# The first quad gathered in one run, score products over 128 rows, no scaling on GpSimd, and another branch at the end, in a two-layer hybrid network on one core

## The chip, the cores and the metric

The kernel runs on one core of a Trainium2 chip. Five engines work side by side: TensorE (PE) multiplies matrices, VectorE (DVE) and ScalarE (ACT) work element by element, GpSimd (POOL) too, and SyncE (SP) issues most of the transfers. The profile calls the queue of an engine PEq, DVEq, ACTq, POOLq and SPq, and the loading of weights into TensorE PEld. The metric is the device time of one execution in microseconds (us), a median over runs.

## The reference

One sequence of 256 tokens, 1024 wide, goes through two layers. Layer 0 mixes with stick-breaking attention and a state-space part, layer 1 with a sparse attention of three branches (compressed blocks, selected blocks, window) and 16 heads; each mixer is followed by a mixture of 16 experts, two of which serve a token, and a layer norm stands behind each step. Cut to what matters here:

```
for layer in range(2):
    m = even_mixer(h, ...) if layer == 0 else nsa_mixer(h, ...)
    h = layer_norm(ALPHA * h + m, ...)
    h = layer_norm(ALPHA * h + moe_ffn(h, ...), ...)

# nsa_mixer, of a head: two of its three branches
p = softmax(mask(q @ ks.T * scale)); o_s = p @ vs
p = softmax(mask(q @ kw.T * scale)); o_w = p @ vw
o = g0 * o_c + g1 * o_s + g2 * o_w

# moe_ffn
for e in range(16):
    y += gates[:, e:e+1] * ((silu(x @ w1[e]) * (x @ w3[e])) @ w2[e])
```

With 256 tokens the selected blocks and the window both cover every earlier token, so the two branches have the same form and differ in their keys and values.

## The kernel before, in words

The kernel runs layer 0's mixer, its experts, layer 1's mixer and its experts, in full precision. Weights come in units of 1 MB (`u` tiles, 128 x 2048), in the order in which they are used; SP issues each as soon as a buffer is free (`issue`, L144). Where a product needs more precision than one pass gives, an operand is split into a rounded part and a remainder (`split`, L192 and L195; `q_turn`, L1396 and L1397; `k_turn`, L1360 and L1362).

**Experts** (`moe`). Each expert has 64 slots. `one_hot` makes a matrix that picks the tokens of four experts (a quad), and `gather` (L469) multiplies the tokens with it, one chunk of 128 features after another: two products of 128x256 to a chunk, and a scaling into `xe` by ScalarE (L354) or VectorE (L356) in turn. `up` (L493) multiplies a quad's slots with the weights of two experts: four products of 128x512 to a chunk and matrix pair, two chunks to a unit. For the first quad the kernel before gathers two chunks, multiplies these, gathers the next two, and so on. Later quads are gathered between other work. `down` (L523) is the second expert product.

**Second attention** (`mixer1`, `head`). For each of 16 heads and each half t of the tokens, three products are added up in PSUM: queries with keys (L1504, 128 rows: 64 features and, under them, the remainders of the same 64 of `qq`), queries with the remainders of the keys (L1505, only the 64 rows of this head's side, `q[s]` and `kl[j][s]`), and the causal mask (L1506). VectorE takes the maximum (L1507), ScalarE the exponential with its sum (L1510), VectorE inverts the sum and multiplies it with the gates (L1513, L1515). Then the probabilities are scaled: for t=0 by VectorE in two pieces of 128x128 (L1522), for t=1 by GpSimd in one piece of 128x512 (L1519; the table `PSC` says which). Two heads later they are transposed (L1529, L1535), copied (L1530, L1536) and multiplied with the values (L1550).

**The end.** The output leaves by four transfers (L348). Then each engine loads a count (L1726) and branches (L1728): if an expert has more tokens than slots, the whole network runs again in a form that copes with any count. This second program stands in the instruction stream between the branch and the common end (L1741), and is not run here. SP's part of it has all the transfers of the second program.

Instructions stand in the order of the program on each engine, except that a scheduler orders VectorE, ScalarE and GpSimd around them by dependences; the stretch after the first quad holds PE to program order.

Of the kernel before, what the change touches and what calls it, by code (L numbers as in the profile page):

```python
# [38 lines left out]
WARM0 = 5  # L39
WARM2 = 2  # L40
LAG = 2
PSC = (lambda h: False, lambda h: True)
OV = 3
LATE = (8, 10)
LATE_S = 11
FIRST = 2
IN_S = 20
CT = (3, 10)
CAP = (5, 9, 19, 20, 10, 14, 12, 10)
# [2 lines left out]
class K:  # L52
# [17 lines left out]
    def restart(self, full):  # L70

        self.full = full
        self.plan, self.tiles, self.late, self.late_s, self.in_s, self.last = [], [], [], [], [], []
        self.left = []
        self.issued = self.used = 0
        self.cap = 0
        self.rest = self.n0 = None
        self.mark = None
        self.loads = None
        self.behind = self.cut = self.tail = None  # L80
        self.staged, self.to_split, self.ahead = [], 0, 2
# [49 lines left out]
    def issue(self, cap=None):  # L131

        self.cap = self.cap if cap is None else cap
        while self.issued < len(self.plan):
            if self.issued - self.used - sum(self.used <= i < self.issued for i in self.left) >= self.cap:
                break
            if self.issued in self.left:
                self.tiles.append(None)
                self.issued += 1
                continue  # L140
            t = (self.s if self.issued in self.in_s else self.u)()
            n = 1024 if self.issued in self.last else 2048
            for c in range(0, 2048, n):
                d = self.loads = self.nc.sync.dma_start(t[:, c:c + n], self.plan[self.issued][:, c:c + n])  # L144
                if self.mark is not None:
                    self.follow(d, self.mark)
            self.tiles.append(t)
            self.issued += 1

    def issue_late(self):  # L150

        i = self.late.pop(0)
        self.tiles[i] = [self.b2() for _ in range(4)]
        for j, t in enumerate(self.tiles[i]):
            self.nc.sync.dma_start(t, self.plan[i][:, j * 512:j * 512 + 512])

    def issue_s(self):

        i = self.late_s.pop(0)
        self.tiles[i] = t = self.s()  # L160
        self.nc.sync.dma_start(t, self.plan[i])

    def unit(self):
        t = self.tiles[self.used]
# [60 lines left out]
    def pack(self, name, dt, parts, t=None):  # L225

        if t is None:
            t = self.const.tile([P, sum(math.prod(sh) for sh in parts)], dt, name="c_" + name)
            setattr(self, name, t)
        d = self.nc.sync.dma_start(t, self.a[name])  # L230
# [107 lines left out]
    def ln_transpose(self, li, n, store=None):  # L338

        nc = self.nc  # L340
        hT = self.u([P, KC, T])
        for k in range(KC):
            pt = self.acc() if k in (4, 5) else self.mm()
            for t in range(2):
                nc.tensor.transpose(pt[:, t * P:(t + 1) * P], n[:, t, k * P:(k + 1) * P], self.ident)
            self.scaled(hT[:, k], pt[:, 0:T], li, k, k % 2)
            if store is not None and k % 2:
                nc.sync.dma_start(store[:, k - 1:k + 1], hT[:, k - 1:k + 1])  # L348
        return hT

    def scaled(self, o, x, li, k, on_act):
# [121 lines left out]
    def moe(self, li, layer, n, hT):  # L473
# [71 lines left out]
                nc.gpsimd.tensor_tensor(nl[:, t], n[:, t], nh[:, t].bitcast(F32), ALU.subtract)  # L545
            return nh, nl

        self.gather(li, G, ns, xe, range(FIRST))
        h1 = self.mm()
        for k in range(0, KC, 2):  # L550
            h1 = up(h1, 0, range(k, k + 2))
            if FIRST + k < KC:
                self.gather(li, G, ns, xe, range(FIRST + k, min(FIRST + k + 2, KC)))
        self.gates(layer)
        rest = []
        with self.tc.manual_schedule(engines=ORD):
# [100 lines left out]
    def s5_tables(self, load_x, room):  # L657
# [7 lines left out]
        nc.sync.dma_start(us[:, 1344:1424], self.a["s5_par"])  # L665
        load_x()
        bc = ua[:, 0:1024].rearrange("p (x a r h) -> p x a r h", x=2, a=NP, r=2)
        nc.sync.dma_start(bc, self.a["s5_bc"])
# [188 lines left out]
    def s5_kernel(self, ca, bd):  # L857

        nc, s5 = self.nc, self.s5
        nc.gpsimd.memset(bd, 0.0)  # L860
        for g in range(2):
            s = slice(g * 64, g * 64 + 64)
            nc.scalar.activation(bd[s, :, :, g * 16:g * 16 + 16], s5["bb"][s], AF.Copy)
        pk = self.mm()
        for k4 in range(4):
            for ri in range(2):
                for q in range(4):
                    pr = k4 * 4 + q
                    nc.tensor.matmul(pk[q * 32:q * 32 + 32, k4 * P:k4 * P + P], bd[:, pr, ri],
                                     ca[ri][:, pr].rearrange("p d h -> p (d h)"), start=(ri == 0), stop=(ri == 1),  # L870
                                     skip_group_check=True, tile_position=(0, q * 32))
        ks = self.b2([P, 4, P])
        nc.scalar.activation(ks.rearrange("p k n -> p (k n)"), pk, AF.Copy)
        nc.gpsimd.tensor_tensor(ks[:, :, 0:16], ks[:, :, 0:16], self.s5dd, ALU.add)
        kds = []
        for kh in range(2):
            kd = self.drp.tile([16, 16, P], F32, name=f"kd{kh}")
            nc.sync.dma_start(kd.rearrange("h (g k) n -> g h (k n)", g=8),
                                ks[:, kh * 2:kh * 2 + 2].rearrange("p k n -> p (k n)"))
            kds.append(kd)  # L880
        return kds

    def s5_toeplitz(self, kds, kts):

        for kt, kd in zip(kts, kds):
            for j in range(8):
                n = 16 * (8 - j)
                self.nc.sync.dma_start(kt[j * 16:j * 16 + 16, :, P - n:P], kd[:, :, 0:n])

    def s5_transpose(self, x, o):  # L890

# [176 lines left out]
    def mixer0(self):  # L1068
# [5 lines left out]

        def load_x():
            t = self.u()
            half = lambda c: nc.sync.dma_start(t[:, c * 1024:c * 1024 + 1024], self.plan[0][:, c * 1024:c * 1024 + 1024])
            for k in range(0, KC, 2):
                nc.sync.dma_start(xT[:, k:k + 2], self.a["xT"][:, k:k + 2])
                if k == 0:  # L1080
                    half(0)
            half(1)
# [18 lines left out]
        def u_out(j):  # L1101
            def f(ps):
                nc.scalar.activation(uS[:, :, j], ps[:, 0:T].rearrange("p (c i) -> p i c", i=8), AF.Copy)
                if j == 3:
                    ud = self.drp.tile([8, P, P], F32, name="ud")
                    nc.sync.dma_start(ud.rearrange("j a n -> a j n"), uS.rearrange("p j k c -> p j (k c)"))
                    nc.sync.dma_start(U.rearrange("p g k c -> p (g k c)"), ud.rearrange("j (h g) n -> (j h) (g n)", h=16))
            return f

        bbp = [self.u([P, 16, 8, 16]) for _ in range(2)]  # L1110
# [190 lines left out]
    def mixer1(self, hT):  # L1301
# [43 lines left out]
        kk = self.u([P, 2, 2, 2, T], F32R)  # L1345
        vh = self.u([P, 2, 1024])
        V = vh[:, 0].rearrange("p (t n) -> p t n", t=2)
        kl = [self.b2((P, 2, T), F32R) for _ in range(2)]
        rows = (slice(0, 64), slice(64, P))

        turned = {}
# [4 lines left out]
        def k_turn(t):  # L1356
            pt = self.turn(turned["k", t]).rearrange("p (b j) n -> p j b n", b=2)
            n = slice(t * P, t * P + P)
            for c, s in enumerate(rows):
                nc.scalar.activation(kk[s, c, :, :, n], pt[s], AF.Copy)  # L1360
                for j in range(2):
                    v.tensor_tensor(kl[j][s, :, n], pt[s, j], kk[s, c, j, :, n].bitcast(F32), ALU.subtract)  # L1362
                nc.scalar.activation(kk[rows[1 - c], c, :, :, n], pt[s], AF.Copy)

        js = [self.job_T(xs, window(i)) for i in (1, 2, 3)] + self.jobs_tok(xs, k_out, self.acc)
# [121 lines left out]
        hd = {}  # L1487

        def head(i, c):
            j, s = i // 4, slice(c * 64, c * 64 + 64)  # L1490
            h = i * 2 + c
# [7 lines left out]
            for t in range(2):  # L1499
# [2 lines left out]
                z3 = z[:, 0:2 * n].rearrange("p (b n) -> p b n", b=2)  # L1502
                q = qq[j][:, c, i % 4, t * P:t * P + P]
                nc.tensor.matmul(z3, q, kk[:, c, j, :, 0:n], start=True, stop=False, skip_group_check=True)  # L1504
                nc.tensor.matmul(z3, q[s], kl[j][s, :, 0:n], start=False, stop=False, skip_group_check=True)  # L1505
                nc.tensor.matmul(z3[:, :, t * P:t * P + P], self.identb, self.caus, start=False, stop=True, skip_group_check=True)  # L1506
                v.tensor_reduce(mx[:, 2 * t:2 * t + 2], z3, AX.X, ALU.max, negate=True)  # L1507
                p_ = self.b2((P, 2, T)) if t else p0
# [5 lines left out]
            s2 = sm.rearrange("p (t b) -> p t b", t=2)  # L1514
            v.tensor_tensor(s2, s2, gt[:, :, h, 1:3], ALU.mult)  # L1515
            for t in range(2):
                x, n, pool = pr[t], P * (t + 1), PSC[t](h)
                if pool:
                    nc.gpsimd.tensor_tensor(x, x, sm[:, 2 * t:2 * t + 2, None].broadcast_to([P, 2, n]), ALU.mult)  # L1519
                    continue  # L1520
                for b in range(2):
                    v.tensor_scalar(x[:, b], x[:, b], sm[:, 2 * t + b:2 * t + b + 1], None, ALU.mult)  # L1522
            hd[h] = (pr, PT)

        def turn_p(h):
# [196 lines left out]
def body(ctx, tc, a, out):  # L1722
# [2 lines left out]
    network(k, a, out)  # L1725
    v = nc.values_load(k.mxi[0:1, 0:1], min_val=0, max_val=T,  # L1726
                       skip_runtime_bounds_check_because="a count of tokens, only compared")
    with tc.If(v > LIMIT):  # L1728

        k.restart(True)  # L1730
        network(k, a, out)
# [20 lines left out]
```

## Time and profile before

| | us |
|---|---|
| median of 3 runs | 756.65 (756.63 to 759.73) |
| profiled execution | 759.68 |
| its span | 757.8 |
| PE busy | 733.8 (97%) |
| DVE busy | 333.1 (44%) |
| ACT busy | 207.5 (27%) |
| POOL busy | 46.8 (6%) |

The span runs from the first to the last instruction of one profiled execution; the time of that execution contains it. The page gives busy time by engine, the span in 40 slices and the costliest groups of instructions with the idle time ahead of them. Here the chain of work that ended last is of no use: it consists of ScalarE's queue alone. More is to be had from the timeline of a stretch, which has the start of each instruction or run of like instructions, and from busy time by stretch.

### The profile page before, as it was taken

How to read it: one execution, taken by the hardware profiler on the slowest of the kernel's cores; microseconds unless marked ns; L12 is line 12 of the kernel's file. 1: busy time of each engine (PE TensorE's matmuls, PEld its weight loads, DVE VectorE, ACT ScalarE, POOL GpSimd, SP SyncE). 2: the span in 40 equal slices, each digit the busy share in tenths (PEclk: the TensorE clock that was granted, in tenths of full speed). 3: DMA queues.
4: the chain of work that ended last, by engine and by line, in shares of the span. 5: the costliest groups of instructions: out<-in, count | busy, mean ns of one | idle time of the engine just before them, and what ended most of it. 6: DMA issues, size and time to landing. Idle time of an engine off the chain costs nothing. (4 is left out here: it accounts for less than half of the span.)

```text
span 757.8 us, 10531 instructions
## 1 busy us (share of the span) xinstructions
PE 733.8 (97%) x4115; PEld 413.9 (55%) x4115; DVE 333.1 (44%) x849; ACT 207.5 (27%) x422; POOL 46.8 (6%) x45
## 2 busy tenths in 40 slices
PE   7999999999999999999999999999999999999993
PEld 6588777634334335334878665687535335343332
DVE  9995667512112112115855897835212112221123
ACT  1345443212101001003534675732211001011002
POOL 2010000002000000000020241300002000000000
PEclk9999999999999999999999998999999999999998
DMA  8838999799999999999982100398799999999941
GB/s 321 299 119 147 398 372 402 256 347 387 381 425 421 421 422 421 420 416 422 420 338 106 57 1 1 135 387 308 233 376 395 393 421 421 422 420 421 421 185 60
DMA packets 42539, 241.00 MB, mean 318 GB/s; under 512 B 8144, under 2 KB 9680, under 8 KB 15568
## 3 DMA queue, kind: packets, MB, share of 16 engines
q1 hardware_dynamic: 42480, 240.23, 80.7%
q8 instruction: 34, 0.56, 0.3%
q14 instruction: 25, 0.20, 0.1%
HBM read 238.38 MB, written 1.84 MB: 317 GB/s over the span
## 5 line engine op out<-in xcount | busy, mean ns | idle before, releaser
L493 PE MATMUL mm<-u,s 128*64 128x512 f32 x960 | 214.3, 595 | 0.0
L493 PEld LDWEIGHTS mm<-u,s 128*64 128x64 f32 x960 | 66.7, 137 | 129.6 <-issue 122.3
L523 PE MATMUL mm<-u,b 128*64 128x512 f32 x512 | 113.1, 593 | 0.0
L528 ACT ACTIVATE b<-mm,gslot 128x512 fp32r<-128x512 f32 x32 | 22.0, 687 | 259.0 <-PE mm L523 259.0
L529 DVE SCALAR_TENSOR_TENSOR b<-mm,gslot,b 128x512 fp32r<-128x512 f32 x32 | 24.0, 751 | 146.2 <-ACT b L528 146.2
L523 PEld LDWEIGHTS mm<-u,b 128*64 128x64 f32 x512 | 36.3, 137 | 72.0 <-issue 70.8
L195 DVE TENSOR_TENSOR s<-u,s 128x1024 fp32r<-128x1024 f32 x37 | 45.8, 1248 | 27.9 <-ACT s L192 26.3
L572 DVE TENSOR_TENSOR b<-b,mm 128x256 f32<-128x256 f32 x32 | 12.0, 417 | 92.0 <-PE mm L493 92.0
L192 ACT ACTIVATE s<-u 128x1024 fp32r<-128x1024 f32 x37 | 38.7, 1056 | 42.0 <-PE acc L205 28.9
L986 PE MATMUL mm<-u,u 128*128 128x256 f32 x208 | 46.7, 382 | 2.5 <-DMA u<-w_in 2.4
L986 PEld LDWEIGHTS mm<-u,u 128*128 128x128 f32 x208 | 38.9, 190 | 9.6 <-issue 2.4
L354 ACT ACTIVATE s<-mm,c_k_all 128x256 f32<-128x256 f32 x32 | 18.1, 564 | 81.8 <-PE mm L469 81.8
L469 PE MATMUL mm<-b,u 128*128 128x256 f32 x160 | 39.0, 325 | 0.0
L203 PE MATMUL acc<-s,u 128*128 128x512 f32 x96 | 38.0, 396 | 0.5 <-ACT u L1206 0.5
L205 PE MATMUL acc<-s,u 128*128 128x512 f32 x96 | 37.8, 394 | 0.0
L204 PE MATMUL acc<-s,u 128*128 128x512 f32 x96 | 37.5, 391 | 0.0
L534 PE MATMUL acc<-b,b 128*128 128x512 f32 x128 | 33.6, 399 | 0.1
L469 PEld LDWEIGHTS mm<-b,u 128*128 128x128 f32 x160 | 29.9, 190 | 6.4 <-issue 4.9
L592 DVE COPY b<-mm 128x512 f32<-128x512 f32 x16 | 11.1, 692 | 46.4 <-PE mm L591 46.2
L356 DVE TENSOR_SCALAR s<-mm,c_k_all 128x256 f32<-128x256 f32 x32 | 16.8, 542 | 22.9 <-PE mm L469 22.7
L534 PEld LDWEIGHTS acc<-b,b 128*128 128x128 f32 x128 | 22.5, 189 | 8.0 <-issue 3.2
L469 PE MATMUL mm<-b,s 128*128 128x256 f32 x96 | 23.5, 286 | 0.0
(312 smaller groups left out, 998.8 us busy)
## 6 DMA issues: line engine op xcount, KB each, us to landing
u<-moe SPq DMA_DIRECT2D x180, 1024.0 KB, 12.5
u<-w_in SPq DMA_DIRECT2D x26, 1024.0 KB, 16.2
u<-w_in SPq DMA_DIRECT2D x10, 512.0 KB, 6.9
s<-moe SPq DMA_DIRECT2D x4, 1024.0 KB, 5.7
b<-moe SPq DMA_DIRECT2D x16, 256.0 KB, 8.1
u<-moe SPq DMA_DIRECT2D x8, 512.0 KB, 16.9
u<-xT SPq DMA_DIRECT2D x4, 256.0 KB, 5.6
out<-u SPq DMA_DIRECT2D x4, 256.0 KB, 4.4
```

The source lines that it names most:

```text
L192: a = self.nc.scalar.activation(s[:, 0], x, AF.Copy)
L195: self.mark = self.nc.vector.tensor_tensor(s[:, 1], x, s[:, 0].bitcast(F32), ALU.subtract)
L203: mm(o, l[0], r[0], start=first, stop=False, skip_group_check=True)
L204: mm(o, l[0], r[1], start=False, stop=False, skip_group_check=True)
L205: self.tail = mm(o, l[1], r[0], start=False, stop=last, skip_group_check=True)
L469: nc.tensor.matmul(pg[:, 0:T], x[:, t, k * P:(k + 1) * P], g.bitcast(F32) if m == 1 else g, start=(i == 0), stop=(i == 2 * m - 1))
L493: self.mark = nc.tensor.matmul(h[c * 64:(c + 1) * 64], xe[:, k, e + c], w[c], start=(k == 0), stop=(k == KC - 1))
L523: self.mark = nc.tensor.matmul(y[c * 64:(c + 1) * 64], hx[:, f, c * 64:(c + 1) * 64], w[:, c * 512:c * 512 + 512], start=(f == 0), stop=(f ...
L528: nc.scalar.activation(yh, y, AF.Copy, scale=gs)
L529: nc.vector.scalar_tensor_tensor(yl, y, gs, yh.bitcast(F32), ALU.mult, ALU.subtract)
L534: self.tail = nc.tensor.matmul(out[half][t], sT[:, t * P:(t + 1) * P], yy, start=False, stop=(p == 7 and j == 1), skip_group_check=True)
L986: self.mark = self.nc.tensor.matmul(ps, w[:, k * P:k * P + P], xT[:, k], start=(k == 0), stop=(k == KC - 1))
```

## The change

Four edits, in the words of the diff. In the expert stage the first quad's eight chunks are gathered in one run, and the eight `up` steps follow. In `mixer1` the remainders of the keys, `kl`, lie in one tile of 128 rows with zeros in the other head's 64 rows (two memsets on GpSimd), so that L1505 runs over all 128 rows; `k_turn`'s subtraction takes both branches at once. `PSC` goes: the probabilities of t=1 are scaled by VectorE, in two pieces of 128x256 for each head. And the second program's transfers are issued by GpSimd's queue (`self.q`), with the branch laid out so that the path that is run here falls through.

```
-PSC = (lambda h: False, lambda h: True)
-FIRST = 2
...
     def restart(self, full):
         self.full = full
+        self.q = self.nc.gpsimd if full else self.nc.sync
...
-                d = self.loads = self.nc.sync.dma_start(t[:, c:c + n], self.plan[self.issued][:, c:c + n])
+                d = self.loads = self.q.dma_start(t[:, c:c + n], self.plan[self.issued][:, c:c + n])
...
-        self.gather(li, G, ns, xe, range(FIRST))
-        h1 = self.mm()
-        for k in range(0, KC, 2):
-            h1 = up(h1, 0, range(k, k + 2))
-            if FIRST + k < KC:
-                self.gather(li, G, ns, xe, range(FIRST + k, min(FIRST + k + 2, KC)))
+        self.gather(li, G, ns, xe, range(KC))
+        h1 = up(self.mm(), 0, range(KC))
...
-        kl = [self.b2((P, 2, T), F32R) for _ in range(2)]
+        kl = self.u([P, 2, 2, 2, T], F32R)
+        for c in range(2):
+            nc.gpsimd.memset(kl[(1 - c) * 64:(1 - c) * 64 + 64, c].bitcast(F32), 0.0)
...
-                for j in range(2):
-                    v.tensor_tensor(kl[j][s, :, n], pt[s, j], kk[s, c, j, :, n].bitcast(F32), ALU.subtract)
+                v.tensor_tensor(kl[s, c, :, :, n], pt[s], kk[s, c, :, :, n].bitcast(F32), ALU.subtract)
...
-                nc.tensor.matmul(z3, q[s], kl[j][s, :, 0:n], start=False, stop=False, skip_group_check=True)
+                nc.tensor.matmul(z3, q, kl[:, c, j, :, 0:n], start=False, stop=False, skip_group_check=True)
...
             for t in range(2):
-                x, n, pool = pr[t], P * (t + 1), PSC[t](h)
-                if pool:
-                    nc.gpsimd.tensor_tensor(x, x, sm[:, 2 * t:2 * t + 2, None].broadcast_to([P, 2, n]), ALU.mult)
-                    continue
                 for b in range(2):
-                    v.tensor_scalar(x[:, b], x[:, b], sm[:, 2 * t + b:2 * t + b + 1], None, ALU.mult)
+                    v.tensor_scalar(pr[t][:, b], pr[t][:, b], sm[:, 2 * t + b:2 * t + b + 1], None, ALU.mult)
...
-    with tc.If(v > LIMIT):
+    with tc.If(v > LIMIT, preferred_fallthrough_block=False):
```

The other `nc.sync.dma_start` of the second program's steps become `self.q.dma_start` in the same way. Line numbers after the change are one to nine lower than before: L469 becomes L468, L493 L492, L1522 L1513, L1530 L1521, L1728 L1719.

PE in the first quad of layer 1's experts before: gather products (two to a row, one chunk) and expert products (four to a row) alternate; `mm_4179` is the first pair of experts, `s_4170` the gathered tokens.

```order
L469 MATMUL mm_4171<-b_730_4167,u_3999 128x256 x2
L469 MATMUL mm_4175<-b_730_4167,u_3999 128x256 x2
L493 MATMUL mm_4179<-u_2800,s_4170 64x512 x4
L469 MATMUL mm_4186<-b_730_4167,u_3999 128x256 x2
L469 MATMUL mm_4190<-b_730_4167,u_3999 128x256 x2
L493 MATMUL mm_4179<-u_2838,s_4170 64x512 x4
L469 MATMUL mm_4200<-b_730_4167,u_3999 128x256 x2
```

The same place after:

```order
L468 MATMUL mm_4184<-b_729_4180,u_4012 128x256 x2
L468 MATMUL mm_4188<-b_729_4180,u_4012 128x256 x2
...
L468 MATMUL mm_4212<-b_729_4180,u_4012 128x256 x2
L492 MATMUL mm_4216<-u_2801,s_4183 64x512 x4
L492 MATMUL mm_4216<-u_2839,s_4183 64x512 x4
L492 MATMUL mm_4216<-u_2961,s_4183 64x512 x4
```

The eight rows of gather products now stand together, ahead of all expert products of the first pair.

DVE in the attention before, around the scalings of one head (`u_3196` its probabilities of t=0, `sm_538` its factors):

```order
L1513 RECIPROCAL sm_538_3198<-sm_538_3198 128x4
L1507 TENSOR_REDUCE mx_544_3229<-acc_3231 128x2
L1515 TENSOR_TENSOR sm_538_3198<-sm_538_3198,b_451_2581 128x4
L1507 TENSOR_REDUCE mx_544_3229<-acc_3238 128x2
L1522 TENSOR_SCALAR u_3196<-u_3196,sm_538_3198 128x128 x2
L1530 COPY u_3136<-mm_3251 128x2x128
```

And after (`b_540` is the head's probabilities of t=1):

```order
L1508 RECIPROCAL sm_537_3197<-sm_537_3197 128x4
L1502 TENSOR_REDUCE mx_543_3229<-acc_3231 128x2
L1510 TENSOR_TENSOR sm_537_3197<-sm_537_3197,b_451_2581 128x4
L1502 TENSOR_REDUCE mx_543_3229<-acc_3238 128x2
L1513 TENSOR_SCALAR u_3195<-u_3195,sm_537_3197 128x128 x2
L1513 TENSOR_SCALAR b_540_3210<-b_540_3210,sm_537_3197 128x256 x2
L1521 COPY u_3133<-mm_3252 128x2x128
```

Two scalings of 128x256 stand behind the two of 128x128; the rows around them keep their order.

SP at the end before: behind the branch stands the second program, with all its transfers.

```order
L1726 TENSOR_LOAD mxi
L1728 COMPARE_AND_BRANCH
L665 DMA u_5312<-s_par 128x80
L1079 DMA u_5306<-xT 128x512
L1077 DMA u_5316<-w_in 128x1024
```

And after:

```order
L1717 TENSOR_LOAD mxi
L1719 COMPARE_AND_BRANCH
L1719 UNCONDITIONAL_BRANCH
L614 COMPARE_AND_BRANCH
L614 UNCONDITIONAL_BRANCH x2
```

A second, unconditional branch follows the first, and what it jumps over on SP holds a loop's control and no transfer.

## Rows read from the trace of the kernel before

**Rows 1.** The page's costly groups: out<-in xcount, busy us, mean ns, idle before.

```profile
L493 PE MATMUL mm<-u,s 128*64 128x512 f32 x960 | 214.3, 595 | 0.0
...
L354 ACT ACTIVATE s<-mm,c_k_all 128x256 f32<-128x256 f32 x32 | 18.1, 564 | 81.8 <-PE mm L469 81.8
```

**Rows 2.** Busy by stretch: us, PE, PEld, DVE, ACT, POOL (instructions), clock, DMA share, GB/s.

```profile
428.00:460.00 32.00, 31.00 (x188) 19.59 (x184) 30.63 (x78) 22.30 (x80) 10.55 (x12) 0.97 0.01 5
460.00:492.00 32.00, 31.77 (x204) 20.21 (x204) 25.98 (x73) 20.59 (x81) 8.98 (x9) 0.92 0.19 73
...
458.00:465.00 7.00, 7.00 (x29) 3.76 (x30) 5.26 (x15) 2.94 (x13) 1.04 (x1) 0.51 0.00 0
```

**Rows 3.** The output's transfers (line L348): ns min/median/max, first and last start.

```profile
L348 SPq DMA_DIRECT2D out<-u x4: 343/376/396, 747.2 to 748.6; - x4
...
DMA to landing us min/median/max: 2.2/4.4/4.5
```

**Rows 4.** SP's instructions of lines L1728 and L1741, the latter by two stretches.

```profile
L1728 SPq EVENT_SEMAPHORE  x8: 17/17/17, 753.3 to 753.8; - x8
...
L1728 SPq COMPARE_BRANCH  x1: 50/50/50, 750.0 to 750.0; - x1
...
L1741 SPq EVENT_SEMAPHORE  x3: 27/28/28, 753.9 to 754.0; - x3
...
L1741 SPq EVENT_SEMAPHORE  x9: 28/28/28, 756.3 to 756.8; - x9
```

**Rows 5.** Timeline around 456 us: start, us, engine, line, in brackets idle before, releaser.

```profile
456.10 0.38 PE L1504 MATMUL acc<-u,u 128*128 128x256 f32 x1 [1.00 <-DVE u L1397]
```

**Rows 6.** Timeline of PE in the first quad of layer 1's experts.

```profile
536.27 1.99 PE L469 MATMUL mm<-b,u 128*128 128x256 f32 x8
...
543.86 1.99 PE L469 MATMUL mm<-b,u 128*128 128x256 f32 x8
```

**Rows 7.** Timeline of PE where either kind runs unbroken.

```profile
545.78 8.80 PE L493 MATMUL mm<-u,s 128*64 128x512 f32 x40
554.41 1.89 PE L493 MATMUL mm<-b,s 128*64 128x512 f32 x8
...
36.03 13.98 PE L986 MATMUL mm<-u,u 128*128 128x256 f32 x64
```

**Rows 8.** Timeline of PE at the scores of one head, t=1 and then t=0.

```profile
448.06 0.48 PE L1504 MATMUL acc<-u,u 128*128 128x512 f32 x1
448.47 0.49 PE L1505 MATMUL acc<-b,u 64*128 64x512 f32 x1
448.90 0.28 PE L1506 MATMUL acc<-c_k_bits 128*128 128x256 bf16 x1
448.93 0.36 PE L1504 MATMUL acc<-u,u 128*128 128x256 f32 x1
449.23 0.38 PE L1505 MATMUL acc<-b,u 64*128 64x256 f32 x1
449.54 0.28 PE L1506 MATMUL acc<-c_k_bits 128*128 128x256 bf16 x1
```

**Rows 9.** Timeline of PE in the output projection behind the attention.

```profile
498.33 0.40 PE L204 MATMUL acc<-s,u 128*128 128x512 f32 x1
498.57 0.39 PE L205 MATMUL acc<-s,u 128*128 128x512 f32 x1
```

**Rows 10.** Groups of DVE and POOL from 424 to 496 us, shapes kept apart.

```profile
L1522 DVE TENSOR_SCALAR u<-u,sm 128x128 f32<-128x128 f32 x32 | 17.9, 593 | 0.1
...
L1519 POOL TENSOR_TENSOR b<-b,sm 128x512 f32<-128x512 f32 x16 | 16.7, 1046 | 47.7 <-DVE sm L1515 36.5 <-ACT u L1536 5.2 <-ACT u L1510 4.1
```

**Rows 11.** Two scalings in DVE's timeline, and line L1062: ns min/median/max, shapes.

```profile
436.74 0.27 DVE L1522 TENSOR_SCALAR u<-u,sm 128x128 f32<-128x128 f32 x1
...
466.54 0.19 DVE L1522 TENSOR_SCALAR u<-u,sm 128x128 f32<-128x128 f32 x1
...
L1062 DVE TENSOR_SCALAR b<-b x3: 295/426/428, 97.2 to 396.8; 128x512 f32<-128x512 f32 x2, 128x256 f32<-128x256 f32 x1
```

More of the change, by code (lines that the diff above doesn't have):

```diff
@@ L154, in issue_late @@
         for j, t in enumerate(self.tiles[i]):
-            self.nc.sync.dma_start(t, self.plan[i][:, j * 512:j * 512 + 512])
+            self.q.dma_start(t, self.plan[i][:, j * 512:j * 512 + 512])
     def issue_s(self):
@@ L160, in issue_s @@
         self.tiles[i] = t = self.s()
-        self.nc.sync.dma_start(t, self.plan[i])
+        self.q.dma_start(t, self.plan[i])
     def unit(self):
@@ L229, in pack @@
             setattr(self, name, t)
-        d = self.nc.sync.dma_start(t, self.a[name])
+        d = self.q.dma_start(t, self.a[name])
         if self.loads is not None:
@@ L347, in ln_transpose @@
             if store is not None and k % 2:
-                nc.sync.dma_start(store[:, k - 1:k + 1], hT[:, k - 1:k + 1])
+                self.q.dma_start(store[:, k - 1:k + 1], hT[:, k - 1:k + 1])
         return hT
@@ L664, in s5_tables @@
         c8 = us[:, 1392:1424]
-        nc.sync.dma_start(us[:, 1344:1424], self.a["s5_par"])
+        self.q.dma_start(us[:, 1344:1424], self.a["s5_par"])
         load_x()
         bc = ua[:, 0:1024].rearrange("p (x a r h) -> p x a r h", x=2, a=NP, r=2)
-        nc.sync.dma_start(bc, self.a["s5_bc"])
+        self.q.dma_start(bc, self.a["s5_bc"])
         lr, li, ldt = par[:, 0], par[:, 1], par[:, 2]
@@ L877, in s5_kernel @@
             kd = self.drp.tile([16, 16, P], F32, name=f"kd{kh}")
-            nc.sync.dma_start(kd.rearrange("h (g k) n -> g h (k n)", g=8),
+            self.q.dma_start(kd.rearrange("h (g k) n -> g h (k n)", g=8),
                                 ks[:, kh * 2:kh * 2 + 2].rearrange("p k n -> p (k n)"))
@@ L887, in s5_toeplitz @@
                 n = 16 * (8 - j)
-                self.nc.sync.dma_start(kt[j * 16:j * 16 + 16, :, P - n:P], kd[:, :, 0:n])
+                self.q.dma_start(kt[j * 16:j * 16 + 16, :, P - n:P], kd[:, :, 0:n])
     def s5_transpose(self, x, o):
@@ L1076, in load_x @@
             t = self.u()
-            half = lambda c: nc.sync.dma_start(t[:, c * 1024:c * 1024 + 1024], self.plan[0][:, c * 1024:c * 1024 + 1024])
+            half = lambda c: self.q.dma_start(t[:, c * 1024:c * 1024 + 1024], self.plan[0][:, c * 1024:c * 1024 + 1024])
             for k in range(0, KC, 2):
-                nc.sync.dma_start(xT[:, k:k + 2], self.a["xT"][:, k:k + 2])
+                self.q.dma_start(xT[:, k:k + 2], self.a["xT"][:, k:k + 2])
                 if k == 0:
@@ L1105, in f @@
                     ud = self.drp.tile([8, P, P], F32, name="ud")
-                    nc.sync.dma_start(ud.rearrange("j a n -> a j n"), uS.rearrange("p j k c -> p j (k c)"))
-                    nc.sync.dma_start(U.rearrange("p g k c -> p (g k c)"), ud.rearrange("j (h g) n -> (j h) (g n)", h=16))
+                    self.q.dma_start(ud.rearrange("j a n -> a j n"), uS.rearrange("p j k c -> p j (k c)"))
+                    self.q.dma_start(U.rearrange("p g k c -> p (g k c)"), ud.rearrange("j (h g) n -> (j h) (g n)", h=16))
             return f
@@ L1489, in head @@
         def head(i, c):
-            j, s = i // 4, slice(c * 64, c * 64 + 64)
-            h = i * 2 + c
+            j, h = i // 4, i * 2 + c
             if c == 0:
```

## The prediction

> **What bounds the kernel now.** I read the costly groups of the page first, then the timelines of the places that the change touches, then busy time by stretch, and the end last. Three things are to be seen. In the expert stages the largest group, the expert products of L493, never waits: 960 matmuls, no idle time ahead of them [rows 1]. Weights are there in time, so TensorE (PE) itself sets the pace, and each microsecond taken from PE there is one off the total. In the second attention (428 to 492 us) PE is busy 31.00 and 31.77 of 32 us in the two halves, and VectorE (DVE) 30.63 and 25.98 [rows 2]. PE sets the pace, but DVE stands 1.4 us behind it in the first half: whatever PE saves there, DVE takes over soon. At the end, the last transfer of the output is issued at 748.6 and lands 4.4 us later (the median), at about 753.1 [rows 3], and the span ends at 757.8: what lies between is SP's queue [rows 4].
>
> [...] Some 7 us at half speed cost up to 3.4 us. The profiled execution took 759.68 us (757.8 of span and 1.9 around it), the median of the three runs 756.65. The difference, 3.03, is close to the cost of that stretch, so I take the median run to be one without it; that is a reading, no row shows a run's clock but this one.
>
> **The first quad's gather.** It removes no instruction. Before, eight gather products (two chunks) alternate with eight expert products. A round takes (543.86 - 536.27) / 2 = 3.80 us [rows 6]. The two kinds alone: 40 expert products unbroken take 554.41 - 545.78 = 8.63 us, so eight take 1.73; 64 f32 products of 128x256, the shape of the gather, take 13.98, so eight take 1.75 [rows 7]. Sum 3.47, so a round pays 0.32 us for going back and forth. Three of the four rounds go, in each of two layers: 6 x 0.32 = 1.9 us, on PE and thus on the path. Bounds: 0, if the first expert product now waits for the last scaling of a chunk (0.56 us on ScalarE [rows 1], every second one on DVE, against 0.87 us of PE per chunk, so hidden but for the last one) and up to 2.2 if the first round, too, had paid more. The first weights come free 5.2 us later (three times 1.75); that L493 never waits says that nothing hangs on it yet.
>
> **Scores over all 128 rows.** L1505 multiplied 64 rows between products over 128. For t=1 (512 columns) the starts stand 0.41, 0.43 and 0.03 us apart, 0.87 in all; for t=0 (256 columns) 0.30, 0.31 and, as for t=1, 0.03, 0.64 in all [rows 8]. Products of 128x512 over 128 rows without such a change follow each other 0.24 us apart [rows 9]. After the change t=1 should cost 0.24 + 0.24 + 0.1 = 0.58. For t=0 half of the columns give 0.12 each, 0.34 in all; if the load of 128x128 weights bounds it, it is 0.2 each and 0.5. Saved per head 0.29 + (0.14 to 0.30), over 16 heads 7 to 9.5 us of PE, about 8. k_turn's eight subtractions become four of twice the width, and two memsets of the zero halves go to POOL; both come before the heads, beside projections that PE runs at its own pace, so I cost them at nothing (at most a microsecond, if PE had to wait for kl).
>
> **POOL's scaling to DVE.** POOL's 16 products over 128x512 (L1519, 1.05 us each, 16.7) go, and DVE gets 32 of 128x256. Of DVE's own 32 scalings (L1522) the mean is 0.593 and the sum 17.9 us [rows 10], but two that run with POOL idle take 0.27 and 0.19 [rows 11]. At their mean of 0.23, 32 cost 7.4, and 10.5 us of DVE come back (9.3 to 11.8 by either). The added 32: the one 128x256 row of this kind has 295 ns [rows 11], so 9.4 us; bounds 0.23 (as much as the half as wide, 7.4) and 0.426 (the twice as wide, 13.6 [rows 11]). I take 9.4, the row of the same shape. Net for DVE -1.1, between -4.4 and +4.3.
>
> So in 428 to 492: PE had 62.8 busy, less 3.4 of slow clock, less 8, is 51.4. DVE had 56.6, now 55.5. The stage, 60.6 without the slow stretch, can't go below 55.5, and of the 5.1 I leave one for waits between two engines that both nearly fill it: the gain is **4.0 us**, not 8. Bounds: 0 (DVE's upper cost gives a floor of 60.9) and 8 (its lower one gives 52.2, near PE's own 51.4). Off the profiled run it is 4.0 + 3.4 = 7.4. What is late next there is DVE: reductions, copies and scalings in turn.
>
> **The end.** SP branches at 750.0 and its next instruction, the first of eight waits, stands at 753.3 [rows 4]. [...] SP's full path held all its DMAs, some 570 instructions, between the branch and its target; now those are POOL's, and SP jumps over some 69. If that short jump stays in code already there, SP reaches its final waits at about 750.2, waits for the last transfer to 753.1, needs 0.3 for the waits behind that one and the 1.0 that the barriers take (from the last of the nine waits at 756.8 to the span's end at 757.8 [rows 4]), and the span ends near 754.4: **3.4 us** less. The other engines jump at the same distance as before and are there by 753.1, so they don't take over by more than tenths. Lower bound 0.5: the eight waits of 0.07 each go and the rest stays.
>
> [...]
>
> Sum against the profiled execution: 759.68 - 7.4 - 1.9 - 3.4 = 747.0; against the median 756.65 - 4.0 - 1.9 - 3.4 = 747.35. I forecast 747.2.
>
> **The rivals.**
> 1. [...]
> 2. *PE's saving carries in full.* [...] Against: 30.63 of 32. All 8 us, 4.0 more than forecast: 743.2.
> 3. [...]
> 4. *The change doesn't do what it says in the attention*: DVE is the bound at once (the added scalings at 0.426) and nothing is gained there, and the end isn't shortened: 747.2 + 4.0 + 2.8 = 754.0.
> 5. *Slower.* One mechanism: PE's waits for DVE are spread over the attention, and the clock falls again and again. At half clock PE's 51 us there become up to 102. Each 7 us costs 3.4; from 747.2 it takes 13.2 us to be slower by over 0.5%, so from four such stretches on, some half of the stage: 760.8. For: DVE will be near 100% there, PE near 90%. Against: at 31.00 and 31.77 of 32 with one such stretch in 64 us [rows 2] the trace shows a single fall, and PE's new waits are spread in tenths, not in one piece.
>
> **How the numbers follow.** Forecast 0.55, rival 1 0.16, rival 2 0.07, rival 3 0.11, rival 4 0.06, slower 0.05. 0.5% is about what a measurement of this kernel can tell from no change: 752.9 and 760.4 are the edges. Forecast and rivals 1 to 3 lie below 752.9 but for their upper tails (0.04): faster 0.85; rival 4 and the tails: same 0.10; slower 0.05. The range, 743.2 to 752.5, takes in the attention from 0 to some 7.5, the end at 0.6 to 3.4 one at a time, and one slow stretch, and leaves out rivals 4 and 5, half of rival 2 and the tails, some 0.2.
>
> **What would show it.** In the first quad of both layers four chunk pairs of gather in a row, and the next expert products 1 us sooner. Score products over 128 rows 0.24 us apart. DVE's scalings at 0.23 and 0.30, the stage of 428 to 492 some 57 us long with DVE over 95% busy and PE near 90%, PE waiting for DVE. SP's last waits in one row at about 753.2, no gap of 2 us. The forecast is wrong if DVE's 128x256 scalings cost over 0.4, if a low clock stands in the attention again, or if SP's code is still fetched behind the jump.

## The result and the profile after

The changed kernel takes 749.33 us (median of four runs, 749.13 to 750.8), against 756.69 for the kernel before: a ratio of 0.989, 95% interval 0.986 to 0.992. The forecast was 747.2 in a range of 743.2 to 752.5. So the sign and the size are as forecast, and 2.1 us of the 9.5 did not come. The profiled execution took 749.13 us, with a span of 747.4. Most kernels here have runs some 1 to 7 us above their fastest group, and the profiles of such runs show a slow stretch in the attention, with the granted clock at about half (0.51 from 458 to 465 us in the profiled run of before, 6.8 us of it slow; 1.00 there in that of the changed kernel), so medians move with the share of such runs, and the parts are better read from the traces.

The page of the changed kernel, lines of the first two of its parts: PE is busy 11.0 us less in a span 10.4 us shorter, of which the slow stretch is some 3, and its granted clock reads 9, that is 90% or more, in every slice.

```profile
span 747.4 us, 10489 instructions
...
PE 722.8 (97%) x4115; PEld 412.6 (55%) x4115; DVE 330.6 (44%) x877; ACT 207.8 (28%) x422; POOL 31.8 (4%) x31
...
PEclk9999999999999999999999999999999999999999
```

**The first quad** (answers to [rows 6, 7]). PE's timeline in layer 1's experts: start, us, engine, line, names, count; below it the first row of the same place in the kernel before.

```profile
526.62 7.07 PE L468 MATMUL mm<-b,u 128*128 128x256 f32 x32
...
533.62 13.95 PE L492 MATMUL mm<-u,s 128*64 128x512 f32 x64
547.41 1.89 PE L492 MATMUL mm<-b,s 128*64 128x512 f32 x8
```

```profile
532.56 1.91 PE L469 MATMUL mm<-b,u 128*128 128x256 f32 x8
```

The eight chunks run in one, and the 64 expert products behind them. From the first gather product to the one behind the 64th expert product it is 547.41 - 526.62 = 20.79 us; before it was 21.85 (532.56 to 554.41). Layer 0 gives the same 1.05.

**The scores** (answers to [rows 8]). PE's timeline at the scores of one head, here t=0 first.

```profile
463.11 0.36 PE L1499 MATMUL acc<-u,u 128*128 128x256 f32 x1
463.31 0.28 PE L1500 MATMUL acc<-u,u 128*128 128x256 f32 x1
463.43 0.28 PE L1501 MATMUL acc<-c_k_bits 128*128 128x256 bf16 x1
463.47 0.48 PE L1499 MATMUL acc<-u,u 128*128 128x512 f32 x1
463.79 0.40 PE L1500 MATMUL acc<-u,u 128*128 128x512 f32 x1
464.02 0.29 PE L1501 MATMUL acc<-c_k_bits 128*128 128x256 bf16 x1
464.17 0.39 PE L1499 MATMUL acc<-u,u 128*128 128x256 f32 x1
```

For t=0 the three starts stand 0.20, 0.12 and 0.04 us apart, 0.36 against 0.64; for t=1 0.32, 0.23 and 0.15, 0.70 against 0.87. That is 0.45 in this head, some 7 us if all 16 are like it, near the lower end of the forecast's 7 to 9.5: t=1 takes 0.70, not 0.58, with 0.32 in place of 0.24 for the product that follows the mask and 0.15 in place of 0.1 at its end.

**The scalings** (answer to [rows 10, 11]). DVE's scalings, durations in ns, min/median/max; then their busy us, mean ns and idle us ahead.

```profile
L1513 DVE TENSOR_SCALAR u<-u,sm x32: 275/279/288, 432.1 to 484.5; 128x128 f32<-128x128 f32 x32
L1513 DVE TENSOR_SCALAR b<-b,sm x32: 343/348/351, 432.5 to 485.0; 128x256 f32<-128x256 f32 x32
...
L1513 DVE TENSOR_SCALAR b<-b,sm 128x256 f32<-128x256 f32 x32 | 9.8, 347 | 0.0
L1513 DVE TENSOR_SCALAR u<-u,sm 128x128 f32<-128x128 f32 x32 | 7.8, 280 | 0.1
```

With GpSimd's products gone, the 128x128 ones no longer spread: 0.28 each, against a mean of 0.593. In the kernel before, 11 of the 32 take 1.03 to 1.07, as long as one of GpSimd's products (1.05); in b3 below, where these products are back, the mean is 0.598 again. Both forms are longer than I took them (0.23 and 0.295). So what DVE lost beside GpSimd's products it now spends on their work: the scalings take DVE 9.8 + 7.8 = 17.6 us, against 17.9.

**The attention as a whole.** To compare equal work, I take the same 492 matmuls in each kernel, from the transposes of the first half of the queries to the output projection (the 2448th to the 2940th of PE). Busy time in the changed kernel, in that stretch and in its two parts, ahead of the compressed branch's second group of products (L1451, the 194th of the 492) and from there on: us, then busy us of PE, PEld, DVE, ACT and POOL (instructions), clock, DMA share, GB/s.

```profile
421.40:499.88 78.48, 72.73 (x494) 52.16 (x493) 62.61 (x191) 51.67 (x171) 4.44 (x5) 1.00 0.28 106
...
421.40:456.10 34.70, 29.95 (x196) 21.20 (x195) 32.34 (x91) 25.27 (x82) 4.44 (x5) 1.00 0.10 31
456.10:499.88 43.78, 42.78 (x299) 30.96 (x300) 30.27 (x101) 26.40 (x90) 0.00 (x0) 1.00 0.42 166
```

The kernel before has 84.4 us for the same work in its profiled run. But that run has the slow stretch. One of the experiments (c3, below) computes what the kernel before computes, in the same order up to its end, and its profiled run has none (1.00):

```profile
421.52:503.05 81.53, 78.96 (x494) 53.27 (x493) 64.78 (x159) 51.90 (x171) 21.19 (x22) 1.00 0.28 108
...
421.52:457.07 35.55, 33.21 (x196) 21.85 (x194) 33.16 (x77) 25.62 (x82) 11.80 (x13) 1.00 0.10 31
457.07:503.05 45.98, 45.75 (x300) 31.42 (x300) 31.62 (x83) 26.28 (x90) 9.38 (x9) 1.00 0.43 167
```

So the slow stretch cost 84.4 - 81.5 = 2.9 us, and the change itself brought 81.53 - 78.48 = 3.05 in the attention, not 4.0. PE's work fell by 6.2 us (78.96 to 72.73), and 3.2 of them turned into waiting: PE was idle 2.6 us before and 5.8 after. DVE's busy time fell by 2.2. Most of the waiting lies in the first part: PE is idle 4.75 of 34.70 us there, and DVE busy 32.34. PE's work in that part fell by 3.3 us and the part by 0.85, which is what DVE's busy time fell by (0.82). In the second part PE is busy 42.8 of 43.8 us and sets the pace as before: its work fell by 3.0 and the part by 2.2. The longest waits of PE in 440 to 460 us, with us in total, times and the longest:

```profile
PE mm L1451 <- DVE u L1393: 1.5, 2, 1.2
...
PE acc L1499 <- DVE u L1393: 0.6, 1, 0.6
```

L1393 is the split of the second half of the queries (`q_turn`), which stands between the heads; DVE does it along with its scalings, and head 8 and the compressed branch's products (L1451) need it. PE waits for ScalarE's exponentials (L1505) too, 0.9 us in this stretch.

**Ahead of the attention.** ScalarE from 399 us, and PE's wait.

```profile
399.40 1.05 ACT L1357 ACTIVATE u<-mm 64x512 fp32r<-64x512 f32 x2
...
404.08 0.59 ACT L1357 ACTIVATE u<-mm 64x512 fp32r<-64x512 f32 x1
...
404.69 0.60 ACT L1441 ACTIVATE u<-mm 128x512 f32<-128x512 f32 x1
...
405.35 0.44 PE L1399 MATMUL mm<-c_k_all,b 128*128 128x128 f32 x2 [0.65 <-ACT u L1441]
```

`k_turn`'s first copies in the kernel before:

```profile
393.33 1.07 ACT L1360 ACTIVATE u<-mm 64x512 fp32r<-64x512 f32 x2 [6.59 <-PE mm L1298]
```

There they stand ahead of ScalarE's next split (399.3); now they come 6 us later, the copy of V (L1441) behind them, and PE waits 0.65 us for it at the transposes of L1399. From the end of layer 0's experts to the attention it takes 0.85 us longer than before. Among the runs below, e3's trace, with the new `kl` alone, has the same loss, and b4's, without it, has none.

**The end** (answers to [rows 3, 4]). SP's branches, its waits, the output's transfers and what SP waits for.

```profile
L1719 SPq COMPARE_BRANCH  x2: 38/46/53, 743.0 to 743.1; - x2
...
L1732 SPq EVENT_SEMAPHORE  x14: 17/28/28, 743.3 to 747.3; - x14
...
L347 SPq DMA_DIRECT2D out<-u x4: 343/398/491, 740.2 to 741.7; - x4
...
DMA to landing us min/median/max: 2.2/3.6/4.5
...
SPq L1732 <- DMA out<-u: 2.5, 2, 1.9
```

The second branch stands at 743.1 and the first wait behind it at 743.3: 0.2 us, where it was 3.3. What SP waits for now are the transfers themselves. From the first transfer's issue to the span's end it is 747.4 - 740.2 = 7.2 us against 757.8 - 747.2 = 10.6: 3.4 less.

The parts sum up: the first quad 2 x 1.05 = 2.1, the end 3.4, the attention 3.05, less 0.85 ahead of it: 7.7, against 7.36 between the medians.

### The profile page after: what moved, and what is told of

It is laid out like the page before. It is cut to its first block, busy times and chain, and to the rows that moved or that the text cites. A ratio compares the mean times of both kernels' runs of the same rounds, so it can differ in the third digit from the quotient of the medians.

```text
span 747.4 us, 10489 instructions
## 1 busy us (share of the span) xinstructions
PE 722.8 (97%) x4115; PEld 412.6 (55%) x4115; DVE 330.6 (44%) x877; ACT 207.8 (28%) x422; POOL 31.8 (4%) x31
## 5 line engine op out<-in xcount | busy, mean ns | idle before, releaser
L492 PE MATMUL mm<-u,s 128*64 128x512 f32 x960 | 213.0, 594 | 0.0
L492 PEld LDWEIGHTS mm<-u,s 128*64 128x64 f32 x960 | 67.2, 137 | 131.0 <-issue 128.7
L468 PE MATMUL mm<-b,u 128*128 128x256 f32 x160 | 37.4, 321 | 0.0
L468 PEld LDWEIGHTS mm<-b,u 128*128 128x128 f32 x160 | 30.4, 191 | 1.7
L468 PE MATMUL mm<-b,s 128*128 128x256 f32 x96 | 23.5, 285 | 0.0
L355 DVE TENSOR_SCALAR s<-mm,c_k_all 128x256 f32<-128x256 f32 x32 | 16.9, 542 | 10.7 <-PE mm L468 10.5
## 6 DMA issues: line engine op xcount, KB each, us to landing
u<-moe SPq DMA_DIRECT2D x8, 512.0 KB, 16.8
```

The costliest lines, as they stand in the source:

```text
L468: nc.tensor.matmul(pg[:, 0:T], x[:, t, k * P:(k + 1) * P], g.bitcast(F32) if m == 1 else g, start=(i == 0), stop=(i == 2 * m - 1))
L492: self.mark = nc.tensor.matmul(h[c * 64:(c + 1) * 64], xe[:, k, e + c], w[c], start=(k == 0), stop=(k == KC - 1))
```

## The experiments

Four runs do one part alone (e1 to e4), two undo one part in the changed kernel (b3, b4), two try a cause and a remedy (b1, b2), three take one mechanism apart (c2 to c4), and c1 joins what worked.

**e1, the gather alone.** The kernel before, with

```
+        self.gather(li, G, ns, xe, range(KC))
+        h1 = up(self.mm(), 0, range(KC))
```

in place of the loop. 

> The kernel before with the first quad's gather in one run, nothing else changed. Theory (going back and forth between gather and expert products costs PE some 0.35 us a round, and PE sets the pace of the expert stages): each of the two layers 1.05 us shorter, so 754.6 us against 756.7, with the first expert products after eight chunks in a row. Rival (the saving is taken back by a later wait for weights or gates): 756.7.

Its median is 757.39 us, ratio 0.999 (0.997 to 1.001): no gain, it seems. But eight of its eleven runs have a mean granted clock of 0.988 to 0.993, among them the profiled one, whose trace has the slow stretch; the other three (0.995 and 0.996) stand at 754.3 to 754.4, 2.1 below the runs of before with such clocks (756.5). In its trace each first quad is 1.04 us shorter, the end 0.5, and all else is as before within 0.2. The theory holds; the median alone would have hidden it.

**e2, the end alone.** The kernel before, with `self.q` and `preferred_fallthrough_block=False`. 

> The kernel before with the second program's transfers on GpSimd's queue and the branch that falls through, nothing else changed. [...] Rival (the end is set by another engine's jump or by the last transfer): 0.6 us less at most, 756.1.

I expected the 3.4 us of the forecast, so 753.3 us: SP's 3.3 us behind its branch and its gap of 2.3 us gone with the long jump.

755.37 us, ratio 0.996 (0.994 to 0.999); five of its twelve runs stand at 753.4 to 753.9. From the first transfer's issue to the span's end it is 755.2 - 747.6 = 7.6 us. So the expected 753.3 holds, the rival's 756.1 does not.

**c2 and c3, which half of the end does it.** c2 has the branch alone:

```
-    with tc.If(v > LIMIT):
+    with tc.If(v > LIMIT, preferred_fallthrough_block=False):
```

> The kernel before with the branch that falls through, the second program's transfers still on SP. [...] Rival (falling through is what saves): 7.1 us.

I expected the time from the first output transfer's issue to the last instruction to stay near the 10.5 us of before, since SP still jumps over some 570 instructions and the length of its jump decides.

c3 has the queue alone:

```
+        self.q = self.nc.gpsimd if full else self.nc.sync
...
-                d = self.loads = self.nc.sync.dma_start(t[:, c:c + n], ...)
+                d = self.loads = self.q.dma_start(t[:, c:c + n], ...)
```

> The kernel before with the second program's transfers on GpSimd's queue, the branch as it was. Theory (the length of SP's jump decides): SP's jump is short, and the time from the first output transfer's issue to the last instruction is near the 7.1 us of the changed kernel. Rival (falling through is what saves): near 10.5 us.

Each ran once, c2 in 763.53 us (mean granted clock 0.988, with two slow stretches, 10.2 us in all, ahead of the end) and c3 in 753.54. c2's waits of SP and its output transfers (span 761.6):

```profile
L1741 SPq EVENT_SEMAPHORE  x14: 17/28/28, 758.5 to 761.5; - x14
...
L1728 SPq EVENT_SEMAPHORE  x8: 17/17/17, 751.9 to 755.2; - x8
...
L348 SPq DMA_DIRECT2D out<-u x4: 343/376/392, 749.0 to 750.4; - x4
```

c3's (span 751.9):

```profile
L1742 SPq EVENT_SEMAPHORE  x14: 17/28/28, 747.4 to 751.8; - x14
...
L349 SPq DMA_DIRECT2D out<-u x4: 343/375/396, 744.4 to 745.8; - x4
```

c3 ends 751.9 - 744.4 = 7.5 us behind the first issue: the queue alone gives the gain. c2 takes 761.6 - 749.0 = 12.6, two more than before: SP now does its eight waits first, for the transfers, until 755.2, and only then makes its long jump, whose first instruction stands at 758.5. So the length of SP's jump decides, and falling through without shortening it is a loss: c2's 12.6 is not the 10.5 that I expected either, as its waits now stand ahead of the jump. The pages count the transfers of code (queue, packets, MB, share). The kernel before, c3, and e4, which follows below:

```profile
q14 instruction: 25, 0.20, 0.1%
...
q14 instruction: 23, 0.19, 0.1%
...
q14 instruction: 24, 0.20, 0.1%
```

The page does not say for which engines they are, but the count goes with the jump: 25 in before, e1, e3 and c2, which have the long one, 24 in e4, 22 or 23 in the nine kernels with the short one. The short jump takes 0.2 us and the long ones 2.8 to 3.3. What SP waits for in the long ones is not shown: in the kernel before, five packets of code (two of q8, three of q14) move between 750.0 and 753.3, and none in the second gap, from 754.0 to 756.3.

**c4, the cost of one round.** The changed kernel with

```
+        for k in range(0, KC, 4):
+            self.gather(li, G, ns, xe, range(k, k + 4))
+            h1 = up(h1, 0, range(k, k + 4))
```

> The changed kernel with the first quad in two rounds: four chunks gathered, their expert products, the other four, theirs. From the first gather product to the end of the 64th expert product layer 1 took 21.85 us in four rounds and 20.79 in one. Theory (each round costs the same 0.35): 21.14. Rival (the cost is that of the first products alone, not of going back and forth): 20.8 or 21.8.

PE's timeline:

```profile
528.82 3.62 PE L468 MATMUL mm<-b,u 128*128 128x256 f32 x16
532.36 3.65 PE L492 MATMUL mm<-u,s 128*64 128x512 f32 x16
535.95 3.72 PE L468 MATMUL mm<-b,u 128*128 128x256 f32 x16
539.60 10.52 PE L492 MATMUL mm<-u,s 128*64 128x512 f32 x48
549.95 1.89 PE L492 MATMUL mm<-b,s 128*64 128x512 f32 x8
```

Its one run took 751.66 us (mean granted clock 0.994), with two slow stretches of 3.4 us in the attention. In the first quad, 549.95 - 528.82 = 21.13: one round 20.79, two 21.13, four 21.85. Each further round costs 0.34 to 0.36. The rows give the two kinds of product as 128*128 and 128*64, and the runs show 0.35 us for going there and back. Whether that difference of the two is the cause, or another, no run here separates.

**e3, the scores alone.** The kernel before with `kl` in one tile and the product over all rows; GpSimd still scales. 

> The kernel before with the score products over all 128 rows (and kl in one tile), the scaling of t=1 still on GpSimd. Theory (DVE is next behind PE and GpSimd's products hold it up as before): 2.5 to 3 us less in the attention, 0.85 lost ahead of it to the later copies of k_turn on ScalarE, so 754.5 to 755.0. Rival (the 32 scalings that DVE got are what capped the gain in the changed kernel): PE's whole 8 us less the 0.85, 749.5.

755.06 us, ratio 0.997 (0.995 to 0.998). The same 492 matmuls:

```profile
422.20:501.79 79.59, 73.70 (x494) 52.10 (x493) 64.38 (x159) 51.85 (x171) 21.18 (x21) 0.98 0.27 106
```

PE's work is 73.70, 5.3 less than the 78.96 of c3 above; the stage is 1.9 shorter, and its profile has a slow stretch of 3.4 us (0.98 for the whole stage), which in c4's and c1's profiles costs 1.0 to 1.4 (80.38 with two of them and 77.90 with one, against 78.48 and 76.46 of the same orders without). So the stage would be some 3 us shorter without it, what the changed kernel gains too. The rival, which put the cap on DVE's added scalings and expected 749.5, falls: with the scalings left on GpSimd the gain is capped as well.

**e4, the scalings alone.** The kernel before with the products over 64 rows, and DVE scaling t=1:

```
-                if pool:
-                    nc.gpsimd.tensor_tensor(x, x, sm[:, 2 * t:2 * t + 2, None].broadcast_to([P, 2, n]), ALU.mult)
-                    continue
```

> The kernel before with the scaling of t=1 on DVE in place of GpSimd, nothing else changed. Theory (PE still sets the pace of the attention, and DVE's sum stays where it was, 17.9 us of scalings before and 17.6 in the changed kernel): no change, 756.7 within 0.5. Rival (DVE without GpSimd's products beside it lets PE run with fewer waits): 755.5 or less.

757.12 us, ratio 1.001 (0.999 to 1.003): the number that the theory gave, for another reason. The same 492 matmuls, and SP's waits at the end:

```profile
421.52:505.60 84.08, 80.84 (x494) 53.90 (x493) 62.82 (x191) 51.83 (x171) 4.43 (x5) 1.00 0.27 104
...
L1736 SPq EVENT_SEMAPHORE  x14: 17/28/28, 753.6 to 755.1; - x14
```

No slow stretch, and yet 84.08 against 81.53: the scalings alone cost 2.5 us of the attention, 1.9 of them as PE's busy time (80.84 against 78.96) and 0.7 as idle time. And the end is 2.5 shorter, 8.1 us from the first transfer's issue: SP's fourteen waits stand without the gap of 2.3 us. SP's transfers are those of the kernel before, its trace has three waits fewer, and the page counts one transfer of code fewer (24). What brings that gap or takes it away no run here shows. Why PE's products take longer with the scalings on DVE was not settled; PE's order changes along with DVE's, and nothing separates them.

**b3 and b4, one part undone in the changed kernel.** b3 takes GpSimd's scaling back (`PSC` as before). 

> The changed kernel with the scaling of t=1 back on GpSimd. [...] Rival (moving the scalings is what brought the gain of the attention): 751.5 or more. Second rival (it cost some): 748 or less.

In runs without a slow stretch I expected it within 1 us of 749.3, since DVE's sum is the same with its own 32 more scalings or with the waits for GpSimd's products (17.6 against 17.9 us).

749.73 us, ratio 0.989 (0.986 to 0.992), with one run at 748.1 and five from 749.7 to 750.3. Its stage:

```profile
420.95:500.64 79.69, 73.80 (x495) 52.05 (x493) 64.39 (x159) 52.02 (x171) 21.17 (x21) 0.98 0.27 107
```

b4 takes the 64 rows back (`q[s]`, `kl[j][s]`). 

> The changed kernel with the score products over 64 rows again (and kl in two tiles). Theory (PE sets the pace again; of PE's 8 us DVE let 2.5 to 3 through): 2.7 lost, 0.85 gained ahead of the attention, so 751.2. Rival (the rows have no part in the gain): 748.5.

755.91 us, ratio 0.997 (0.994 to 0.999), from 753.8 to 759.0. The expected 751.2 does not hold even for its fastest runs.

b3 holds: over 128 rows it hardly matters for the attention who scales. b3's profile has a slow stretch of 3.4 us, so 79.69 is 78.3 to 78.7 without it, the changed kernel's 78.48. Its one run at 748.1 is 1.0 below the fastest of the changed kernel (749.13): giving the scalings to DVE brought nothing here, and whether it cost something, one run can't tell. b4's fastest runs agree with e4: 84.08 in place of 78.48 is 5.6 more, less the 0.85 ahead of the attention, 749.1 + 4.75 = 753.9. So the two edits do not add up: with the scalings on GpSimd the 128 rows gain some 3.1, with the scalings on DVE 5.6; the scalings cost 2.5 with 64 rows and about nothing with 128.

**b2, is DVE's sum the pace?** The changed kernel with L1521 on ScalarE:

```
-            v.tensor_copy(PT[:, :, 0:P], pt[:, 0:T].rearrange("p (b n) -> p b n", b=2))
+            nc.scalar.activation(PT[:, :, 0:P], pt[:, 0:T].rearrange("p (b n) -> p b n", b=2), AF.Copy)
```

> The changed kernel with the 16 copies of L1521 (128x256, 0.41 us each, 6.6 us in all) on ScalarE in place of DVE. Theory (DVE sets the pace of the attention after the change): the stage falls towards PE's own length, 3 to 5 us less, 744.5 to 746.5. Rival (waits between the engines in turn, not DVE's sum, set the pace): within 1 us of 749.3, or slower, since ScalarE's chain of exponentials gets longer.

747.7 us, ratio 0.987 (0.984 to 0.990).

```profile
421.14:497.60 76.46, 72.04 (x495) 52.10 (x494) 57.86 (x175) 56.17 (x187) 4.61 (x5) 1.00 0.29 114
```

DVE's work falls by 4.75 us (62.61 to 57.86), the stage by 2.0 (78.48 to 76.46), and PE's idle time from 5.8 to 4.4. The theory expected 3 to 5 and the rival less than 1: it lies between. Split at the same product as above, the first part falls from 34.70 to 34.04 us with 1.0 less of DVE, the second from 43.78 to 42.42 with 3.75 less. So DVE holds PE up in both; a microsecond off DVE brings some 0.65 where DVE is nearly full and 0.36 where PE is.

**b1, a remedy that failed.** The changed kernel with

```
-        nc.scalar.activation(hid, ph[:, 0:256], AF.Copy)
+        self.follow(nc.scalar.activation(hid, ph[:, 0:256], AF.Copy), self.k_act)
```

where `k_act` is the last of `k_turn`'s first copies. 

> The changed kernel with one more rule of order: the copy of hid on ScalarE stands behind k_turn's first copies, as the kernel before had them. Theory (the 0.85 us lost ahead of the attention come from k_turn's copies, 6 us later on ScalarE than before, which hold PSUM tiles that the compressed branch waits for): 0.85 less than the changed kernel's 749.3, so 748.5. Rival (DVE takes the 0.85 back in the attention, or the loss has another cause): 749.3.

751.26 us, ratio 0.991 (0.988 to 0.994): 2 us more than the changed kernel, where 0.85 less was expected; in its trace 0.83 of it lies ahead of the attention and 0.3 in it; the profiled run took 749.98, so the rest is not in this trace. PE at the transposes of `hid`:

```profile
399.75 0.41 PE L1399 MATMUL mm<-c_k_all,b 128*128 128x128 f32 x2 [1.32 <-DVE b L1061]
```

`k_turn` did come early, at 392.3, but `hid` and the gelu behind it (L1061) now came late, and PE, which has these transposes earlier in its order here, waited 1.32 us for them in place of 0.65 for V's copy. So the rule on `hid` exchanged one wait for another; it says nothing yet on the cause.

**c1, another remedy, and the best version.** b2 with the next split, not `hid`, tied behind `k_turn`'s first copy:

```
+        k_acts = []
...
-                nc.scalar.activation(kk[s, c, :, :, n], pt[s], AF.Copy)
+                k_acts.append(nc.scalar.activation(kk[s, c, :, :, n], pt[s], AF.Copy))
...
+        self.behind = k_acts[0]
```

> The changed kernel with the 16 copies of L1521 on ScalarE (which gave 747.7 alone) and with the next split on ScalarE behind k_turn's first copy. Theory (the 0.85 us lost ahead of the attention come from ScalarE's order around k_turn, where the copies of V and with them PSUM tiles came too late): some 0.85 less than with the copies alone, 746.9, and no idle stretch of PE ahead of the compressed branch's transposes. Rival (any other order of ScalarE there costs the same, as the rule on hid's copy did): 747.7 or more.

746.9 us (746.2 to 747.9), ratio 0.987 (0.985 to 0.989). ScalarE and PE at the same place:

```profile
393.92 1.05 ACT L1358 ACTIVATE u<-mm 64x512 fp32r<-64x512 f32 x2
...
402.73 0.60 ACT L1443 ACTIVATE u<-mm 128x512 f32<-128x512 f32 x1 [0.47 <-PE mm L204]
...
403.67 0.38 PE L1401 MATMUL mm<-c_k_all,b 128*128 128x128 f32 x2
```

V's copy now waits for PE and not PE for it, and the stretch from the end of layer 0's experts to the attention is 0.87 shorter, what was lost. So the loss was ScalarE's order around `k_turn`. This version beats both kernels: all of its runs lie below all of the changed one's, 2.4 us by the medians. The copies give some 2.0 in the attention and the order 0.87; its profiled run has a slow stretch of 3.4 us (0.98 for the whole stage), and its interval overlaps b2's, so the second part is shown by the trace rather than by the medians.

## Why the prediction was right, and where it was not

**The first quad**: forecast 1.9, measured 2.1. Right, and c4 shows the price per round (0.35; I had 0.32). No later wait took it back, as L493's zero idle had said.

**The end**: forecast 3.4, measured 3.4. Right in that the short jump does it, as c3 shows; with the long one c2 still waits 3.2 us behind its branch (755.3 to 758.5). That SP would find its code there and stand at its final waits 0.2 us behind the short jump, at 750.2, was my estimate. No run shows what fills the two gaps of before; what the changed kernel shows is the 0.2 us, and no second gap.

**Ahead of the attention**: I costed `k_turn` and the memsets at nothing, at most a microsecond if PE had to wait for `kl`. It cost 0.85, but not through `kl`: the scheduler put `k_turn`'s copies 6 us later on ScalarE, and what came behind them on that engine, V's copy, was late for PE. The step that failed is "beside projections that PE runs at its own pace": I had looked at what the moved work needs, not at what stands behind it in its queue, though the order of ScalarE was there to read.

**The attention**: forecast 4.0, measured 3.05 (2.9 more went with the slow stretch, which I had put at up to 3.4, from 7.00 us at 0.51 [rows 2]). PE's saving of about 8 measured 6.2 as busy time. The cap was named rightly, but its working was wrong: I compared DVE's sum over 64 us with PE's and took the larger as the floor, with one microsecond for waits. Neither engine fills the stage throughout. Up to 456 us, with `q_turn` among its work, DVE is nearly full (32.3 of 34.7) and the saving, 0.85, is no more than DVE's own; behind it PE is the pace (42.8 of 43.8) and 2.2 of its 3.0 come through. The mis-sized term is that one microsecond of waits. The stretch that I had summed, 60.6 us without the slow clock (61.2 in c3), is now that from 427.5 to 485.3 us, with as many products, ten of them others: 57.8 us, DVE busy 53.9 and PE 53.4. DVE is idle for 3.9, not 1. That the gain there, 3.4, is still near 4.0 is partly luck, for DVE's sum fell below the 55.5 that I had forecast. DVE was to be over 95% busy and PE near 90%: it is 93% and 92%. DVE's scalings cost more than estimated each, 17.6 us in all and not 16.8, because I averaged a 128x128 row of 0.27 with one of 0.19, and in the trace of the kernel before no other of the 32 is under 0.27; why DVE's busy time in the stage still fell by 2.2 and not by 1.1 is open.

**The rivals.** The first (SP as late behind its jump as before, 750.0 us) and the second (PE's saving in full) fell. The third, a slow stretch in each run (750.6), fell for the changed kernel's profiled run, though its slowest run (750.8) may have one; it is what most runs of b3 and some of the others show. The fourth and the fifth fell: PE waits for DVE more often than before, and its granted clock stayed at 1.00 throughout the attention of the profiled run.

## What to carry to other kernels

Where two engines nearly fill a stage, split it into stretches before taking the larger sum as the floor: what is saved on one engine turns into waits wherever the other is full, and the rest of the stage pays most. When an edit moves work in a scheduler's order, read what is then queued behind it on that engine, and who waits for that. And at the end of a program, look at how far the last jump goes: the transfers of a path that isn't taken cost 3.4 us here by lying in between.

## What the runs showed that I had not expected

Two edits that cost or gain alone do otherwise together: scaling on DVE cost 2.5 us with products over 64 rows and nothing over 128 (e4, b3, b4); the cause is open. The granted clock fell to about half behind waits of PE of 1.0 us (the kernel before, 0.51 from 458 to 465 us, in some runs and not in others: c3's trace has the same wait and 1.00 throughout) and of 1.4 us (c1), yet the changed kernel's trace has one of 1.2 us and 1.00 behind it, and c2's falls for 3.4 us at 374.8 with no wait of PE shown in the 10 us ahead, so the waits alone don't tell. A stretch of 6.8 us at half speed cost 2.9 us, not 3.4, one of 3.4 us between 1.0 and 1.4. And SP's second gap, of 2.3 us, was gone in e4, an edit that does not touch the end: a median that stays the same can hide a gain of 2.5 and a loss of 2.5.
